# Two-layer decoder trunk on one core: expert positions in another order, overflow branch behind slot group 9 instead of 13

## Chip, cores and metric

One core of a Trainium2 chip runs the whole program. The metric is the device time of one execution in microseconds (us); the median of the runs is quoted. TensorE is PE in the profile (its weight loads PEld), VectorE DVE, ScalarE ACT, GpSimd POOL; SP is SyncE, whose queue issues all weight transfers here.

## The reference, cut to what matters

A trunk of two layers works on x (256 tokens x 1024). Layer 0 mixes with dilated attention and gated spatial mixing, layer 1 with a convolution module and stick-breaking attention; behind each mixer stands the same mixture of experts, and this is the part that the change touches:

```python
g_prob = softmax(x @ w_group + b_group)            # 4 groups, the best one is taken
e_val, e_idx = top_k(e_logits_of_that_group, 2)    # 2 of its 4 experts
gates = one_hot(group * 4 + e_idx) * (g_w * softmax(e_val))
for e in range(16):
    hid = silu(xt @ w_gate[e]) * (xt @ w_up[e])    # 1024 -> 512
    y = y + gates[:, e:e+1] * (hid @ w_down[e])    # 512 -> 1024
```

256 tokens with two experts each make 512 (token, expert) pairs for 16 experts. All is float32: the three matrices of one expert are 6 MB, those of both layers 192 MB.

## The kernel before

**Positions and slot groups.** The kernel sorts the experts of a layer by how many tokens chose them. Positions 0 and 1 are always experts 0 and 1 (`FIXED`), positions 2 to 15 the others, most chosen first. Each position has a fixed capacity of slots (`CAP`: 96 for positions 0 to 3, 64 for 4 to 7, 32 for 8 to 15; 896 in all). `_tasks()` goes through the positions and cuts their slots into slot groups of 64 or 32, 20 of them, numbered 0 to 19, and every 128 slots make a pack (7 packs). A position of 96 has two slot groups (64 and 32, or 32 and 64), the others have one each.

**A slot group** `i` goes through these steps, and the main loop of `moe_layer` overlaps neighbours: `prepare` copies its tokens into a window (ACT); `first_half` and `second_half` multiply the window with the gate and up matrices, 512 rows of them each (PE, L132 with `win` or `hs`); `hidden` makes silu(gate)*up*weight (ACT L1338, DVE L1339); `turn` transposes it (PE L1345, ACT L1347); `project` multiplies with the down matrix (PE, L132 with `ht`) and splits the result into two parts (ACT L1475, DVE L1476). When a pack is full, `combine` adds it to the tokens with matmuls (`ptt`, `yp`). Step `i` of the loop issues on PE: first half of `i+1`, `combine` where a pack has just ended, `turn` of `i`, second half of `i+1`, `project` of `i`.

**The ring of weights.** All big matrices of the program come as pieces of 1 MB (128 x 2048 float32) in a fixed order, `order`: four gate and up pieces and two down pieces for each position, 96 per expert layer. `moe()` writes this order from `TASKS`. The pieces go into 15 buffers (`raw`), and a few more tiles that are idle in this stage serve as buffers once (`pump_extra`). A piece is issued on SP (L248) when a buffer is free; a buffer is free when PE has done its last work with the piece, so the pieces of a position of 96 stay until its second slot group. SP issues in program order. The pieces of positions 0 and 1 can come before the routing is known; those of position 2 and on wait until the routing has told which expert stands there (L245).

**The overflow branch.** If an expert has more tokens than its capacity, the excess must be worked on apart. `whatever_is_left` reads the number of such tokens into a register of each engine (L1399) and goes into a branch (L1400) if it is over zero; the branch (`further`) loads the weights of that expert again, into tiles of its own. Its place is behind `project` of slot group `LEFT`, 13. In the profiled execution no engine goes into it, but each engine jumps past its code. In step 13 alone, `next_window` (the window copy of `i+2`, and the placing of its pack) stands behind the branch; in other steps it stands ahead of `project`.

Of the kernel before, what the change touches and what calls it, by code (L numbers as in the profile page):

```python
# [10 lines left out]
F32 = mybir.dt.float32  # L11
F32R = mybir.dt.float32r
# [7 lines left out]
P = 128  # L20
D = 1024
KD = 8
S = 256
# [13 lines left out]

FIXED = 2
CAP = (96,) * 4 + (64,) * 4 + (32,) * 8
PLAN = [[(0, 5), (1, 0), (1, 1)], [], [(1, 2), (1, 3), (1, 4), (1, 5)], []]  # L40
OD_ORDER = (0, 1, 2, 3, "2", 4, 5, 6, 7, "3", "4", 8, 9, "5", 10, 11, 12, 13)
HK = 1
# [2 lines left out]
AGE = 3  # L45
ADA_PE = {(0, 1), (1, 3), (1, 4), (1, 5)}
EXTRA = ("f8", "m8")
LEFT = 13
WARM = (1, 8, 8, 2, 4, 4, 3)


# [12 lines left out]
def _tasks():  # L64

    out, at = [], 0
    for p, cap in enumerate(CAP):
        base = 0
        while base < cap:
            n = 64 if cap - base >= 64 and at % 64 == 0 else 32  # L70
            out.append(dict(p=p, base=base, n=n, pack=at // P, row=at % P, first=base == 0, last=base + n == cap))
            base += n
            at += n
    assert at % P == 0
    return out


TASKS = _tasks()
# [31 lines left out]
def trunk_kernel(ctx: ExitStack, tc: tile.TileContext, a, out, dbg=None):  # L110
    nc = tc.nc
    V, A, G, T = nc.vector, nc.scalar, nc.gpsimd, nc.tensor
# [3 lines left out]
    sb = ctx.enter_context(tc.tile_pool(name="act", bufs=1))  # L116
# [5 lines left out]
    def bank(i):  # L122
        return pp.tile([P, 512], F32, name=f"b{i}", tag=f"b{i}")
# [327 lines left out]
    for i in range(4):  # L451
        b = bank(i)
# [820 lines left out]
    def place(rr, e, base, G):  # L1273

        pe = sb.tile([P, 2, P], BF, name="pe", tag="pt")
        for t in range(2):
            V.tensor_scalar(pe[:, t, :].rearrange("p (g w) -> p g w", g=G),
                            iota[:, 0:P // G].unsqueeze(1).to_broadcast([P, G, P // G]),
                            rr[:, t, e:e + 1], float(-base), op0=OP.subtract, op1=OP.is_equal)
        return pe  # L1280

    def moe_layer(l, then):
# [21 lines left out]
        with in_order():  # L1304
            g3, rr, hs, ofi, exi, pe = route(l, wa, cb, lg, th, tl, sm)

        def load_window(o, base, n):
            w = sb.tile([P, KD, n], F32, name="win", tag="sq", bufs=3)
            A.copy(w, hs[:, :, ds(o + base, n) if base else ds(o, n)])  # L1309
            return w  # L1310

        def slots(e, base, pe):
            b = bankbf(7)
            g = b[:, 512:518].bitcast(F32)
            for t in range(2):
                mm(g, pe[:, t, :], g3[:, t, e, :], start=(t == 0), stop=(t == 1))
            for t in range(2):
                T.transpose(b[:, t * P:(t + 1) * P], pe[:, t, :], identb)
            gs = sb.tile([P, 1], F32, name="gs", tag="gs1")
            V.tensor_reduce(gs, g, AX.X, OP.add)  # L1320
            ptt = sb.tile([P, S], F32R, name="ptt", tag="rs")
            A.copy(ptt, b[:, 0:S])
            return ptt, gs


        def gate_up(w, wts, b, G, halves=(0, 1)):
            n, r = DE // G, P // G
            for h in [x for f in halves for x in (2 * f, 2 * f + 1)]:
                i, src = h % 2, k3(wts[h], 4)
                for kk in range(4):  # L1330
                    for g in range(G):
                        mm(b[g * r:(g + 1) * r, i * n:(i + 1) * n], w[:, h // 2 * 4 + kk, :],
                           src[:, kk, g * n:(g + 1) * n], start=(h + kk == 0), stop=(h + kk == 6))

        def hidden(b, gs, G, tag="hid"):
            n = DE // G
            hid = sb.tile([P, n], F32, name="hid", tag=tag)
            A.activation(hid, b[:, 0:n], AF.Silu)  # L1338
            V.scalar_tensor_tensor(hid, hid, gs, b[:, n:2 * n], op0=OP.mult, op1=OP.mult)  # L1339
            return hid  # L1340

        def turn(hid, b, G, tag="ht"):
            n, m = DE // G, DE // G // P
            for c in range(m):
                T.transpose(b[:, c * P:(c + 1) * P], hid[:, c * P:(c + 1) * P], ident)  # L1345
            ht = sb.tile([P, m, G, P // G], F32, name="ht", tag=tag)
            A.copy(ht.rearrange("p c g s -> p (c g s)"), b[:, 0:n])  # L1347
            return ht

        def down(ht, wts, G):  # L1350
            n, r, m, q = D // G, P // G, DE // G // P, KD // G
            y = bank(6)
            for j in range(4):
                src = k3(wts[j // 2], 2)[:, j % 2, :].rearrange("p (n k) -> p n k", k=KD)
                for g in range(G):
                    mm(y[g * r:(g + 1) * r, 0:n], ht[:, j % m, j // m, :], src[:, :, q * g:q * (g + 1)],
                       start=(j == 0), stop=(j == 3))
            return y
# [5 lines left out]
        def further(p, base, bk):  # L1364

            def load(name, tag, cut):
                r = sb.tile([P, 2048], F32, name="raw", tag=tag)
                e = p if p < FIXED else nc.sync.value_load(exi[0:1, p:p + 1], min_val=0, max_val=NE - 1)
                nc.sync.dma_start(k3(r, 4 if name != "moe_w_down" else 2), cut(a[name][l, e]))
                return r  # L1370

            tags = ("f8", "m8", "m8b", "r8")
            wts = []
            for h in range(2):
                for name in ("moe_w_gate", "moe_w_up"):
                    wts.append(load(name, tags[len(wts)],
                                    lambda w: w.rearrange("(p k) n -> p k n", k=KD)[:, 4 * h:4 * h + 4, :]))
            b = bank(bk)
            pt, gs = slots(p, base, place(rr, p, base, 2))
            o = nc.scalar.value_load(ofi[0:1, 16 + p:17 + p], min_val=0, max_val=2 * S - base)  # L1380
            gate_up(load_window(o, base, 64), wts, b, 2)
            ht = turn(hidden(b, gs, 2, "m8b"), b, 2, "r8")
            wts = [load("moe_w_down", tags[h], lambda w: w.rearrange("(j p) n -> p j n", p=P)[:, 2 * h:2 * h + 2, :])
                   for h in range(2)]
            y = down(ht, wts, 2)
            for n in range(2):
                yx = sb.tile([P, 512], F32R, name="yx", tag="sq", bufs=3)
                A.copy(yx, y)
                if n:
                    V.tensor_sub(yx, y, yh.bitcast(F32))  # L1390
                yh = yx
                for kk in range(4):
                    for g in range(2):
                        k, rows = 4 * g + kk, slice(64 * g, 64 * g + 64)
                        mm(acc[k // 2][:, (k % 2) * S:(k % 2 + 1) * S],
                           yx.rearrange("p (n k) -> p k n", k=4)[rows, kk, :], pt[rows, :])
# [10 lines left out]
        start, banks, wins, gates, packs, hid, gu, dw_ = {}, {}, {}, {}, {0: pe}, {}, {}, {}  # L1407
        n = len(TASKS)

        def prepare(i):  # L1410
            t = TASKS[i]
            if t["p"] == 0:
                wins[i] = hs[:, :, t["base"]:t["base"] + t["n"]]
                return
            if t["first"]:
                start[t["p"]] = nc.scalar.value_load(ofi[0:1, 16 + t["p"]:17 + t["p"]], min_val=0, max_val=2 * S)
            wins[i] = load_window(start[t["p"]], t["base"], t["n"])
# [77 lines left out]
        for i, t in enumerate(TASKS):  # L1495
            if i + 1 < n:
                first_half(i + 1)
            if i and TASKS[i - 1]["pack"] < t["pack"]:
                combine(t["pack"] - 1)
            ht = turn(hid.pop(i), banks.pop(i), P // t["n"])  # L1500
            if i + 1 < n:
                gate_of(i + 1)
                second_half(i + 1)
            def next_window():
                if i + 2 < n:
                    prepare(i + 2)
                    j = TASKS[i + 2]["pack"]
                    if j > TASKS[i + 1]["pack"]:
                        packs.pop(j - 2, None)
                        packs[j] = place_pack(rr, j)  # L1510
                        return j

            if i != LEFT:
                j = next_window()
            project(i, ht)
            if i == LEFT:

                whatever_is_left(4 + i % 2)
                j = next_window()
            if j:  # L1520
                ptts[j] = turned_pack(j)
            if st["fin"]:
                ada_flush(7, -1)
# [14 lines left out]
    h = rms(drain_ada)  # L1538
# [81 lines left out]
```

## Time and profile before

| what | value |
|---|---|
| median of 3 runs | 855.37 us (850.36, 855.37, 857.51) |
| the profiled execution's own time | 853.71 us |
| its span, first to last instruction | 851.9 us (1.8 us lie around it) |
| PE busy | 710.1 us, 83% |
| DVE, ACT busy | 375.1 us (44%), 236.2 us (28%) |
| bytes moved by DMA | 288.11 MB, mean 338 GB/s |
| mean granted TensorE clock | 0.908 of 2.4 GHz |

Busy times of different engines overlap and don't add up to the span. The clock is granted at one of two levels, 1.2 or 2.4 GHz; a figure between is the mean of a stretch. The program runs in this order: layer 0 mixer to about 184 us, its experts to about 429 us, layer 1 mixer and routing to about 592 us, its experts to about 831 us, final norm and output.

### The profile page before, as it was taken

To read this page: it belongs to the slowest core of one execution; us is meant where nothing else is said; L and a number is where in the kernel's file an instruction comes from. 1 tells how busy PE (TensorE), PEld (TensorE's weight loads), DVE (VectorE), ACT (ScalarE), POOL (GpSimd) and SP (SyncE) were. 2 spreads that over 40 slices of the span, in tenths; PEclk is the share of its full clock that TensorE was granted. 3 is DMA by queue.
4 is the path that set the end of the run, shared out by engine and by line. 5 is a ranking of instruction groups with operands and counts; after the bars stand their busy time and mean duration, and the time that the engine had idled before them with its cause. 6 is when DMAs were issued, how large, how long until landed. Compare 5 with 4: busy or idle time off the path is not lost. (4 is left out here: it accounts for less than half of the span.)

```text
span 851.9 us, 18148 instructions
## 1 busy us (share of the span) xinstructions
PE 710.1 (83%) x7597; PEld 486.8 (57%) x7597; DVE 375.1 (44%) x852; ACT 236.2 (28%) x532; POOL 13.2 (2%) x33
## 2 busy tenths in 40 slices
PE   3699899889999997566638999997999999836666
PEld 2366369856665555443328887884666556524333
DVE  2435788883222122111157999997322212202113
ACT  3111241032232122211145336463222312111113
POOL 0000020000000000000000000000000000000000
PEclk9799999989999998775678999999999999976757
DMA  8999999949789999989999995501997699999981
GB/s 312 351 314 400 400 409 415 414 167 386 281 310 346 421 413 418 411 354 418 402 398 351 375 416 211 198 1 57 421 407 269 231 421 414 416 409 363 418 359 50
DMA packets 70027, 288.11 MB, mean 338 GB/s; under 512 B 8909, under 2 KB 11273, under 8 KB 53544
## 3 DMA queue, kind: packets, MB, share of 16 engines
q1 hardware_dynamic: 69928, 286.77, 85.6%
q8 instruction: 64, 1.05, 0.5%
q14 instruction: 35, 0.29, 0.1%
HBM read 285.69 MB, written 1.06 MB: 337 GB/s over the span
## 5 line engine op out<-in xcount | busy, mean ns | idle before, releaser
L132 PE MATMUL b<-raw,win 128*32 128x128 f32 (+1 forms) x3712 | 206.9, 323 | 36.2 <-ACT win L1309 19.1
L132 PEld LDWEIGHTS b<-raw,win 128*32 128x32 f32 (+1 forms) x3712 | 147.0, 126 | 88.7 <-ACT win L1309 20.5
L132 PE MATMUL b<-raw,ht 128*32 128x256 f32 (+1 forms) x1024 | 122.2, 505 | 28.8 <-DMA raw<-in_moe_w_down_dram 21.7
L1476 DVE TENSOR_TENSOR yp<-b,yp 32x256 fp32r<-32x256 f32 (+1 forms) x128 | 62.4, 488 | 166.9 <-ACT yp L1475 166.8
L1475 ACT CAST yp<-b 32x256 fp32r<-32x256 f32 (+1 forms) x128 | 53.5, 418 | 160.5 <-PE b L132 120.2
L132 PEld LDWEIGHTS b<-raw,ht 128*32 128x32 f32 (+1 forms) x1024 | 43.2, 128 | 87.6 <-issue 47.0
L310 DVE SCALAR_TENSOR_TENSOR raw<-raw,csil 128x1024 f32<-128x1024 f32 x56 | 74.6, 1332 | 4.2 <-DMA raw<-in_w_ada_dram 3.2
L1339 DVE SCALAR_TENSOR_TENSOR hid<-hid,gs,b 128x128 f32<-128x128 f32 (+1 forms) x40 | 16.0, 401 | 112.0 <-ACT hid L1338 111.9
L132 PE MATMUL b<-hh,whf 128*128 128x256 f32 x160 | 40.8, 294 | 13.2 <-ACT whf L601 13.1
L887 DVE SCALAR_TENSOR_TENSOR ac<-hqk,dw,ac 128x256 f32<-128x256 f32 x120 | 50.4, 476 | 0.2
L132 PE MATMUL b<-h,raw 128*128 128x256 f32 x192 | 44.9, 393 | 5.5 <-ACT h L574 2.9
L132 PEld LDWEIGHTS b<-h,raw 128*128 128x128 f32 x192 | 37.2, 197 | 13.3 <-ACT h L574 3.8
L1338 ACT ACTIVATE hid<-b 128x128 f32<-128x128 f32 (+1 forms) x40 | 12.8, 321 | 104.8 <-PE b L132 104.8
L132 PE MATMUL b<-mx,raw 128*128 128x256 f32 x160 | 40.8, 410 | 0.0
L132 PEld LDWEIGHTS b<-mx,raw 128*128 128x128 f32 x160 | 38.8, 335 | 1.5 <-issue 1.2
L132 PEld LDWEIGHTS b<-hh,whf 128*128 128x128 f32 x160 | 28.9, 194 | 17.5 <-ACT whf L601 15.2
L132 PE MATMUL b<-ptt,yp 128*128 128x256 f32 x224 | 34.3, 306 | 3.3 <-ACT yp L1475 3.1
L132 PE MATMUL b<-hl,whf 128*128 128x256 f32 x128 | 36.6, 286 | 0.0
L1437 DVE TENSOR_REDUCE gs<-b 128x1 f32<-128x3 f32 x40 | 6.4, 161 | 67.8 <-PE b L132 67.5
L132 PEld LDWEIGHTS b<-ptt,yp 128*128 128x128 f32 x224 | 30.2, 204 | 9.5 <-ACT yp L1475 6.0
L1347 ACT COPY ht<-b 128x128 f32<-128x128 f32 (+1 forms) x40 | 12.3, 309 | 77.3 <-PE b L1345 77.2
L132 PE MATMUL b<-raw,h 128*128 128x512 f32 x64 | 30.9, 631 | 0.0
(285 smaller groups left out, 821.4 us busy)
## 6 DMA issues: line engine op xcount, KB each, us to landing
raw<-in_moe_w_gate_dram SPq DMA_DIRECT2D x64, 1024.0 KB, 10.6
raw<-in_moe_w_up_dram SPq DMA_DIRECT2D x64, 1024.0 KB, 11.6
raw<-in_moe_w_down_dram SPq DMA_DIRECT2D x64, 1024.0 KB, 16.8
raw<-in_w_ada_dram SPq DMA_DIRECT2D x48, 1024.0 KB, 14.2
raw<-in_ev_w_in_dram SPq DMA_DIRECT2D x10, 1024.0 KB, 13.5
raw<-in_od_w_in_dram SPq DMA_DIRECT2D x10, 1024.0 KB, 8.3
raw<-in_ev_w_out_dram SPq DMA_DIRECT2D x4, 1024.0 KB, 16.0
raw<-in_od_w_out_dram SPq DMA_DIRECT2D x4, 1024.0 KB, 11.3
```

Source lines behind the costliest of these rows:

```text
L132: T.matmul(o, l, r, start=start, stop=stop, skip_group_check=True)
L310: ins = V.scalar_tensor_tensor(acc, src, csil[:, k:k + 1], acc, op0=OP.mult, op1=OP.add)
L887: V.scalar_tensor_tensor(ac[:, m, :], src, dw[:, m, j:j + 1], ac[:, m, :], op0=OP.mult, op1=OP.add)
L1338: A.activation(hid, b[:, 0:n], AF.Silu)
L1339: V.scalar_tensor_tensor(hid, hid, gs, b[:, n:2 * n], op0=OP.mult, op1=OP.mult)
L1347: A.copy(ht.rearrange("p c g s -> p (c g s)"), b[:, 0:n])
L1437: V.tensor_reduce(gates[i], g, AX.X, OP.add)
L1475: A.copy(yh[o[0], o[1], :], src)
L1476: V.tensor_sub(yl[o[0], o[1], :], src, yh[o[0], o[1], :].bitcast(F32))
```

## The change

`SEQ` gives the order in which the positions are worked on; `_tasks()` follows it, and with it the order of the pieces, the packs and the slot groups. There are 20 slot groups and 7 packs as before, of the same sizes. The new list of slot groups is, by position and size: 0 (64, 32), 1 (32, 64), 8 (32), 9 (32), 2 (64, 32), 10 (32), 3 (64, 32), 11, 12, 13 (32 each), 4, 5, 6, 7 (64 each), 14, 15 (32 each). `place_pack` writes a pack with one DVE instruction when all its positions are whole, equal and consecutive; that held for four packs before and holds for one in the new order, so the 7 packs take 19 such instructions per layer instead of 12.

The branch goes from behind slot group 13 to behind slot group 9, which is the first of position 3. `next_window` is gone: window copy and placing of a pack stand ahead of `project` in every step. Inside the branch the tiles are arranged anew, so that none of them is one of the windows' tiles.

```diff
--- before.py
+++ after.py
@@ -37,6 +37,8 @@
 
 FIXED = 2
 CAP = (96,) * 4 + (64,) * 4 + (32,) * 8
+
+SEQ = (0, 1, 8, 9, 2, 10, 3, 11, 12, 13, 4, 5, 6, 7, 14, 15)
 PLAN = [[(0, 5), (1, 0), (1, 1)], [], [(1, 2), (1, 3), (1, 4), (1, 5)], []]
 OD_ORDER = (0, 1, 2, 3, "2", 4, 5, 6, 7, "3", "4", 8, 9, "5", 10, 11, 12, 13)
 HK = 1
@@ -45,7 +47,7 @@
 AGE = 3
 ADA_PE = {(0, 1), (1, 3), (1, 4), (1, 5)}
 EXTRA = ("f8", "m8")
-LEFT = 13
+LEFT = 9
 WARM = (1, 8, 8, 2, 4, 4, 3)
 
 
@@ -64,7 +66,8 @@
 def _tasks():
 
     out, at = [], 0
-    for p, cap in enumerate(CAP):
+    for p in SEQ:
+        cap = CAP[p]
         base = 0
         while base < cap:
             n = 64 if cap - base >= 64 and at % 64 == 0 else 32
@@ -1304,8 +1307,8 @@
         with in_order():
             g3, rr, hs, ofi, exi, pe = route(l, wa, cb, lg, th, tl, sm)
 
-        def load_window(o, base, n):
-            w = sb.tile([P, KD, n], F32, name="win", tag="sq", bufs=3)
+        def load_window(o, base, n, tag=None):
+            w = sb.tile([P, KD, n], F32, name="win", tag=tag or "sq", bufs=1 if tag else 3)
             A.copy(w, hs[:, :, ds(o + base, n) if base else ds(o, n)])
             return w
 
@@ -1369,26 +1372,27 @@
                 nc.sync.dma_start(k3(r, 4 if name != "moe_w_down" else 2), cut(a[name][l, e]))
                 return r
 
-            tags = ("f8", "m8", "m8b", "r8")
+            tags = ("f8", "m8", "f8", "m8")
             wts = []
             for h in range(2):
                 for name in ("moe_w_gate", "moe_w_up"):
                     wts.append(load(name, tags[len(wts)],
                                     lambda w: w.rearrange("(p k) n -> p k n", k=KD)[:, 4 * h:4 * h + 4, :]))
-            b = bank(bk)
-            pt, gs = slots(p, base, place(rr, p, base, 2))
-            o = nc.scalar.value_load(ofi[0:1, 16 + p:17 + p], min_val=0, max_val=2 * S - base)
-            gate_up(load_window(o, base, 64), wts, b, 2)
-            ht = turn(hidden(b, gs, 2, "m8b"), b, 2, "r8")
+                if h == 0:
+                    b = bank(bk)
+                    pt, gs = slots(p, base, place(rr, p, base, 2))
+                    o = nc.scalar.value_load(ofi[0:1, 16 + p:17 + p], min_val=0, max_val=2 * S - base)
+                    w = load_window(o, base, 64, "m8b")
+                gate_up(w, wts, b, 2, (h,))
+            ht = turn(hidden(b, gs, 2, "r8"), b, 2, "m8b")
             wts = [load("moe_w_down", tags[h], lambda w: w.rearrange("(j p) n -> p j n", p=P)[:, 2 * h:2 * h + 2, :])
                    for h in range(2)]
             y = down(ht, wts, 2)
+            y2 = sb.tile([P, 2, 512], F32R, name="y2", tag="r8")
+            A.copy(y2[:, 0, :], y)
+            V.tensor_sub(y2[:, 1, :], y, y2[:, 0, :].bitcast(F32))
             for n in range(2):
-                yx = sb.tile([P, 512], F32R, name="yx", tag="sq", bufs=3)
-                A.copy(yx, y)
-                if n:
-                    V.tensor_sub(yx, y, yh.bitcast(F32))
-                yh = yx
+                yx = y2[:, n, :]
                 for kk in range(4):
                     for g in range(2):
                         k, rows = 4 * g + kk, slice(64 * g, 64 * g + 64)
@@ -1501,22 +1505,17 @@
             if i + 1 < n:
                 gate_of(i + 1)
                 second_half(i + 1)
-            def next_window():
-                if i + 2 < n:
-                    prepare(i + 2)
+            j = 0
+            if i + 2 < n:
+                prepare(i + 2)
+                if TASKS[i + 2]["pack"] > TASKS[i + 1]["pack"]:
                     j = TASKS[i + 2]["pack"]
-                    if j > TASKS[i + 1]["pack"]:
-                        packs.pop(j - 2, None)
-                        packs[j] = place_pack(rr, j)
-                        return j
-
-            if i != LEFT:
-                j = next_window()
+                    packs.pop(j - 2, None)
+                    packs[j] = place_pack(rr, j)
             project(i, ht)
             if i == LEFT:
 
                 whatever_is_left(4 + i % 2)
-                j = next_window()
             if j:
                 ptts[j] = turned_pack(j)
             if st["fin"]:
```

## Rows read from the trace of the kernel before

**Rows 1.** The page: the span.
```profile
span 851.9 us, 18148 instructions
```

**Rows 2.** Windows: stretch, length; busy PE, PEld, DVE, ACT, POOL; PEclk, DMA, GB/s.
```profile
219.00:288.00 69.00, 69.00 (x811) 41.61 (x809) 14.59 (x35) 16.68 (x42) 0.00 (x0) 1.00 0.86 330
...
362.00:385.00 23.00, 14.45 (x238) 9.17 (x241) 2.55 (x7) 2.57 (x8) 0.20 (x1) 0.75 0.91 360
...
448.00:592.00 144.00, 135.37 (x1029) 111.46 (x1029) 129.74 (x300) 71.30 (x135) 1.02 (x2) 0.99 0.59 228
...
631.00:682.00 51.00, 51.00 (x664) 31.37 (x664) 11.98 (x29) 13.95 (x35) 0.00 (x0) 1.00 0.74 279
682.00:744.00 62.00, 59.30 (x792) 36.64 (x788) 12.85 (x28) 12.70 (x31) 0.00 (x0) 1.00 1.02 416
...
765.00:795.00 30.00, 17.54 (x356) 12.85 (x355) 5.78 (x18) 4.30 (x13) 0.00 (x0) 0.75 0.95 380
795.00:828.00 33.00, 21.29 (x343) 12.19 (x339) 5.63 (x15) 5.36 (x17) 0.00 (x0) 0.66 1.01 409
```

**Rows 3.** Waits of SP in 631 to 682 us: total, times, longest.
```profile
SPq L248 <- PE b L132: 40.5, 11, 16.8
```

**Rows 4.** SP's timeline in layer 1: start, duration, issue of a piece.
```profile
631.17 0.33 SPq L248 DMA_DIRECT2D raw<-in_moe_w_up_dram  x1
644.44 0.33 SPq L248 DMA_DIRECT2D raw<-in_moe_w_gate_dram  x1
...
650.57 0.35 SPq L248 DMA_DIRECT2D raw<-in_moe_w_up_dram  x1
667.97 0.33 SPq L248 DMA_DIRECT2D raw<-in_moe_w_gate_dram  x1
```

**Rows 5.** ACT's timeline, layer 1: silu of slot groups 3, 4, 5, 9, 10, 11, 13, 14, 19.
```profile
631.17 0.38 ACT L1338 ACTIVATE hid<-b 128x256 f32<-128x256 f32 x1 [3.41 <-PE b L132]
...
642.73 0.39 ACT L1338 ACTIVATE hid<-b 128x256 f32<-128x256 f32 x1 [3.25 <-PE b L132]
...
650.58 0.28 ACT L1338 ACTIVATE hid<-b 128x128 f32<-128x128 f32 x1 [1.53 <-PE b L132]
...
692.40 0.39 ACT L1338 ACTIVATE hid<-b 128x256 f32<-128x256 f32 x1 [3.25 <-PE b L132]
...
703.69 0.38 ACT L1338 ACTIVATE hid<-b 128x256 f32<-128x256 f32 x1 [3.25 <-PE b L132]
...
716.55 0.39 ACT L1338 ACTIVATE hid<-b 128x256 f32<-128x256 f32 x1 [3.25 <-PE b L132]
...
733.98 0.28 ACT L1338 ACTIVATE hid<-b 128x128 f32<-128x128 f32 x1 [1.64 <-PE b L132]
...
740.41 0.28 ACT L1338 ACTIVATE hid<-b 128x128 f32<-128x128 f32 x1 [1.40 <-PE b L132]
...
819.50 0.28 ACT L1338 ACTIVATE hid<-b 128x128 f32<-128x128 f32 x1 [3.51 <-PE b L132]
```

**Rows 6.** Line L1400 in 740 to 790 us: ns min/median/max, first and last start.
```profile
L1400 SPq EVENT_SEMAPHORE  x7: 17/17/17, 766.3 to 780.9; - x7
L1400 PEldq COMPARE_BRANCH  x2: 81/3437/6793, 745.0 to 745.8; - x2
```

**Rows 7.** Timelines of SP and PE around the branch in layer 1.
```profile
784.36 1.03 SPq L248 DMA_DIRECT2D raw<-in_moe_w_down_dram  x2
...
755.41 2.78 PE L132 MATMUL b<-raw,win 128*32 128x128 f32 x45 [9.96 <-ACT win L1309]
```

**Rows 8.** PE's timeline in layer 0: half a slot group of 32 at either clock.
```profile
347.99 3.64 PE L132 MATMUL b<-raw,win 128*32 128x128 f32 x64 [9.13 <-ACT win L1309]
...
356.48 1.96 PE L132 MATMUL b<-raw,win 128*32 128x128 f32 x64
```

**Rows 9.** Timeline, 408 to 462 us: first issues and first use of layer 1's mixer weights.
```profile
403.96 16.41 SPq L248 DMA_DIRECT2D raw<-in_od_w_in_dram  x4
...
447.96 2.17 ACT L601 CAST whf<-raw 128x512 fp32r<-128x512 f32 x4
```

## Prediction

> **What bounds the kernel now.** I read the windows first, for the weight transfers and PE side by side, then SP's waits and its timeline, then the spacing of the slot groups on ACT, then the branch. A layer's experts need 96 pieces of 1.049 MB. Where nothing holds the transfers they run at 416 GB/s (682 to 744 [rows 2]), so a piece takes 1.049 MB / 416 GB/s = 2.52 us and a position (six pieces) 15.1 us, whatever its capacity.
>
> PE's price of a position depends on its capacity. The silu marks the end of a slot group's second half, so its spacing is PE's time per slot group [rows 5]: 740.41 - 733.98 = 6.4 us for a 32, 703.69 - 692.40 = 11.3 us for a 64, and 650.58 - 631.17 = 19.4 us for a position of 96 (two slot groups). A `combine` adds 12.9 - 11.3 = 1.6 us (716.55 - 703.69 against the spacing before it). So a 96 costs PE 4.3 us more than its transfer, a 64 costs 3.8 us less, a 32 costs 8.7 us less. All four 96s stand at the front. There the ring of buffers fills and SP waits for PE to empty one: of the 51 us from 631 to 682, SP waits 40.5 us for PE's matmuls [rows 3], and the issues stop from 631.17 to 644.44 and, after eight pieces (644.44 to 650.57), until 667.97 [rows 4]. PE is busy all the time, transfers run at 279 GB/s [rows 2]. Behind the 96s it turns round: transfers are full, PE waits for pieces, and the transfers set the end. So transfer time lost at the front is never made good. At 416 GB/s the loss is 51 x (1 - 279/416) = 16.8 us in layer 1, and 69 x (1 - 330/416) = 14.3 us in the same stretch of layer 0 (219 to 288) [rows 2]: 31.1 us together.
>
> **The change part by part.** *The order.* Number of pieces, slot groups, their sizes and PE's work stay. Slot groups 0 to 3 (positions 0, 1) are the same, so everything up to 631.17, the silu of slot group 3, should stand where it is. Then come positions 8 and 9, two 32s, instead of position 2. I follow the buffers in layer 1. Silu of slot group 4: 6.4 + 1.6 (a `combine` falls here) = 8.0 us later, 639; of slot group 5, a 32 that follows a projection of 64, 650.58 - 642.73 = 7.9 us [rows 5], 647. A piece of gate and up is free with its half of the matmuls, a piece of down with the projection behind. So by 649 free: four of position 8, two (down) of position 1, four of position 9, two of position 8: 12 pieces, the first about 636. Position 9's down and position 2's gate and up make 18 by about 665. Before, only eight were freed by then, and the next at 667.97 [rows 4]. The pieces issued up to 631.17 keep the queue busy to about 641 (four of 2.52 us from there), 12 more to 671, 18 to 686: the queue never runs dry. Afterwards position 2 and 10 take PE 19.4 + 6.4 = 25.8 us for 12 pieces that need 30.2 us, so do 3 and 11, and 12 and 13 are 32s: PE gains on the transfers all the time. I take off 31.1 us, and give back 1 us for a short hole that may be left about 640 in both layers: -30 us. The bounds of this term: all of it gone, and with it the holes at the branch (5.7 us, below), -37; or half of it left, -16.
>
> *Does PE become the bound?* From 631.2 PE has, in the new order, eight 32s (51 us), two 96s (39), four 64s (45), six `combine`s (9) and the branch (7): 151 us, so the last silu could stand at 783. The transfers allow it 16 to 17 us ahead of the 819.50 of before [rows 5], at about 803. The slack is 20 us; the end stays with the transfers, and the tail behind the last piece has the same two positions, 14 and 15, in it as before.
>
> *The branch* is moved past four slot groups. PE pays 6.8 us for its second compare-and-branch [rows 6] and stood 9.96 us in all, because the window copy came behind ACT's branch [rows 7]; with the window ahead of it I take 7. What is queued behind is slot group 11 and the buffers it frees; by then some six pieces (15 us) are queued or in flight, more than 7, so this hides. If that cover were gone it would cost 7 us a layer. On SP the branch waits from 766.3 until 780.9 for transfers in flight [rows 6], and SP issues again at 784.36 [rows 7], 3.4 us later. The transfers fall to 380 GB/s in 765 to 795 and 360 in 362 to 385 [rows 2]: a hole of 30 x (1 - 380/416) = 2.6 us and 23 x (1 - 360/416) = 3.1 us. All pieces behind are queued behind that wait. No row shows the branch where fewer transfers are in flight: at best the hole vanishes (-2.6 us a layer), at worst SP stands 3.4 us with nothing in flight and then the first piece takes its own 2.52 us: 6 us, 3.4 more than now. I take no difference, as the nearest rows, on both sides of the change, have a filled queue.
>
> *The rest.* `place_pack` has seven DVE instructions more per layer, DVE is busy 12 of 51 us there [rows 2], and PE needs the pack a slot group later: nothing. Without that cover, 7 x 0.41 us (11.98 us for 29 instructions) = 2.9 us a layer. The new tiles in the branch are not run.
>
> *Does layer 0's gain last?* Layer 1's mixer is bound by PE (135 of 144 us busy, transfers at 228 GB/s [rows 2]). Its first weights are issued from 403.96 on and first used at 447.96 [rows 9], so both its transfers and its start move ahead together with the end of layer 0's experts. I count it in full.
>
> Sum: 853.7 - 30 = 824 us for an execution like the profiled one (span 851.9 [rows 1], so about 822); the median shown is 1.7 us higher, within the spread of its own three runs. I predict 824.
>
> **The rivals.** (1) *The clock falls behind the 64s.* Positions 4 to 7 now stand where PE waits for pieces. In those stretches the granted clock averages 0.75 and 0.66, in the full ones 1.00 [rows 2], and at the lower level, 1.2 GHz, half a slot group of 32 took 3.64 instead of 1.96 us [rows 8], 1.86 times as much. At 1.86 a 64 costs 21.0 us and a 32 11.9: four 64s and the last two 32s lose 39 + 11 = 50 us, the last silu comes at 833 instead of 819.50, and the kernel takes 853.7 + 2 x 13.5 = 881 us. It turns slower from 20 + 17 = 37 us lost per layer, that is about three quarters of this stretch at the lower level. For it: such means were measured there. Against it: they were measured with PE busy 18 of 30 and 21 of 33 us; 64s ask for 11.3 of 15.1 us at the full clock, all of it at the lower one, and stretches with 59.3 of 62 us busy or more had 1.00 [rows 2]. The Trainium skill ("TensorE: Matmul & The Clock Gate", section "HAM oscillation — how this bites in real kernels") speaks for this rival: it says that PE whose bursts alternate with long waits for DMA is throttled again and again and starts each burst at the low clock. By that rule alone the 881 would stand; the trace agrees with it for 32s and has no 64 in such a stretch.
>
> (2) *The branch costs in its new place.* If the queue is short at that time, PE's 7 us and SP's hole add up to 7 us a layer, so half the gain: 853.7 - 16 = 838. For it: it comes where PE has just left the front. Against it: the count of 18 pieces by 665.
>
> (3) *The gain stays in one layer,* because the mixer between absorbs it: 853.7 - 16 = 838. Against it: the order of events above.
>
> (4) *The change does not do what it says:* the transfers lose the same time elsewhere, because the ring refills with later pieces while something else on PE (evacuation at the pack ends, say) holds the buffers: 853 to 856. Against it: rows 3 put the waits on matmuls.
>
> **How the numbers follow.** The forecast gets 0.72, rival 1 0.08, rival 2 0.10, rival 3 0.04, rival 4 0.06. The forecast's own range is 817 to 831 (-37, to -30 with 3.4 us a layer given back at the branch). Rivals 1 and 4 are left out (0.14); with rivals 2 and 3 in, and 2 us at either end because single runs differ by that much and more, the range that should hold 8 in 10 is 815 to 840. A change under 1% (8.5 us) is about what a measurement of this kernel can't tell from none. Faster by over 1% are the forecast, rivals 2 and 3: 0.86; the same, rival 4: 0.06; slower, rival 1: 0.08.
>
> **What would show it.** The forecast is right if the stretch that follows slot group 3 runs at 405 GB/s or more in both layers, SP's waits for matmuls there shrink to a few us, PE first waits for pieces only from position 4 or 5 on, and routing of layer 1 comes some 14 us earlier. Rival 1 shows as a clock near 0.5 in positions 4 to 7 with PE full and SP waiting for it again. Rival 2 shows as a dip of the transfers right at the branch. The step that I trust least is the count of freed buffers about 640: if slot groups 4 and 5 come later than 649, holes remain.

## The result and the profile after

The changed kernel took 824.05 us (median of 4 runs, 823.33 to 827.35), the kernel before 852.96 in the runs beside it: ratio 0.9663, 95% interval 0.9607 to 0.9719. The profiled execution has a span of 821.9 us, 30.0 less than [rows 1]. So the forecast of 824 holds, and the 30 us can be followed by stage.

The windows of the changed kernel (columns as in [rows 2]) in the order of time, layer 0 first; the stretches 219 to 274 and 617 to 668 answer to 219 to 288 and 631 to 682 of before:

```profile
219.00:274.00 55.00, 54.75 (x915) 35.79 (x913) 13.93 (x40) 15.03 (x41) 0.00 (x0) 1.00 1.02 415
274.00:312.00 38.00, 30.23 (x621) 21.86 (x618) 8.35 (x21) 9.38 (x26) 0.00 (x0) 0.91 0.94 374
...
617.00:668.00 51.00, 50.77 (x882) 33.67 (x876) 13.75 (x38) 14.71 (x40) 0.00 (x0) 1.00 1.02 409
668.00:692.00 24.00, 15.35 (x250) 10.19 (x247) 4.93 (x13) 4.24 (x11) 0.00 (x0) 0.85 1.01 410
692.00:712.00 20.00, 19.18 (x427) 14.73 (x430) 4.89 (x14) 5.66 (x16) 0.00 (x0) 0.84 0.87 348
712.00:730.00 18.00, 18.00 (x221) 10.71 (x215) 4.98 (x15) 5.61 (x15) 0.00 (x0) 1.00 1.02 415
730.00:751.00 21.00, 19.45 (x142) 10.25 (x140) 2.58 (x6) 3.59 (x9) 0.00 (x0) 1.00 1.02 416
751.00:781.00 30.00, 22.47 (x256) 11.98 (x253) 3.82 (x8) 3.88 (x9) 0.00 (x0) 1.00 1.02 416
```

Behind slot group 3 the transfers are full: 415 GB/s for 330 and 409 for 279 [rows 2]. PE is as busy there as before (54.75 of 55 and 50.77 of 51 us). What is left is one dip per layer, at the branch (374 and 348).

SP's timeline shows that the long stops of [rows 4], 13.3 and 17.4 us, are gone: the longest left is 8.8 us, from 635.06 to 643.85 (start, duration, issue; first the first piece behind the routing, then pieces that follow slot group 3):

```profile
577.59 0.35 SPq L251 DMA_DIRECT2D raw<-in_moe_w_gate_dram  x1
...
619.82 0.35 SPq L251 DMA_DIRECT2D raw<-in_moe_w_gate_dram  x1
...
635.06 0.33 SPq L251 DMA_DIRECT2D raw<-in_moe_w_up_dram  x1
643.85 3.24 SPq L251 DMA_DIRECT2D raw<-in_moe_w_down_dram  x4
650.52 0.35 SPq L251 DMA_DIRECT2D raw<-in_moe_w_gate_dram  x1
```

ACT's silus of slot groups 3, 4, 5 and 19 of layer 1 answer to [rows 5]:

```profile
616.96 0.38 ACT L1341 ACTIVATE hid<-b 128x256 f32<-128x256 f32 x1 [3.41 <-PE b L135]
625.58 0.28 ACT L1341 ACTIVATE hid<-b 128x128 f32<-128x128 f32 x1 [1.53 <-PE b L135]
633.23 0.28 ACT L1341 ACTIVATE hid<-b 128x128 f32<-128x128 f32 x1 [1.69 <-PE b L135]
...
789.53 0.28 ACT L1341 ACTIVATE hid<-b 128x128 f32<-128x128 f32 x1 [3.82 <-PE b L135]
```

In the kernel before, the first piece of position 2 in layer 1, which marks the end of the routing, went out here (SP's timeline):

```profile
591.85 0.36 SPq L248 DMA_DIRECT2D raw<-in_moe_w_gate_dram  x1
```

So layer 1's routing ends 591.85 - 577.59 = 14.3 us earlier, which is layer 0's part. From there to the last silu the kernel before took 819.50 - 591.85 = 227.7 us [rows 5], the changed one 789.53 - 577.59 = 211.9, which is 15.7 us less. Together this is the 30.0 us of the span.

### The profile page after: what moved, and what is told of

Its sections match the earlier page's. It is cut to its first block, busy times and chain, and to the rows that moved or that the text cites. A ratio compares the mean times of both kernels' runs of the same rounds, so it can differ in the third digit from the quotient of the medians.

```text
span 821.9 us, 18157 instructions
## 1 busy us (share of the span) xinstructions
PE 703.7 (86%) x7597; PEld 485.0 (59%) x7597; DVE 375.6 (46%) x866; ACT 236.1 (29%) x532; POOL 13.2 (2%) x33
## 5 line engine op out<-in xcount | busy, mean ns | idle before, releaser
L135 PE MATMUL b<-raw,win 128*32 128x128 f32 (+1 forms) x3712 | 200.3, 310 | 35.5 <-issue 17.9
L135 PEld LDWEIGHTS b<-raw,win 128*32 128x32 f32 (+1 forms) x3712 | 142.4, 121 | 85.5 <-issue 27.3
L135 PE MATMUL b<-raw,ht 128*32 128x256 f32 (+1 forms) x1024 | 116.8, 475 | 19.3 <-DMA raw<-in_moe_w_down_dram 13.2
L135 PE MATMUL b<-ptt,yp 128*128 128x256 f32 x224 | 36.4, 306 | 3.9 <-ACT yp L1479 2.9
L1350 ACT COPY ht<-b 128x128 f32<-128x128 f32 (+1 forms) x40 | 12.3, 308 | 86.6 <-PE b L1348 86.5
## 6 DMA issues: line engine op xcount, KB each, us to landing
raw<-in_w_ada_dram SPq DMA_DIRECT2D x48, 1024.0 KB, 14.3
```

The lines of the kernel that those rows point to most:

```text
L135: T.matmul(o, l, r, start=start, stop=stop, skip_group_check=True)
```

## The experiments

All of them start from the changed kernel, and each ratio is to the kernel before, in runs on the same chip.

**The order alone.**

```diff
-LEFT = 9
+LEFT = 13
```

> The new order with the branch back behind slot group 13. Theory (the ring, held by PE in the front, starved the transfers; the order alone cures it): 821 to 827 us, the stretch behind slot group 3 as full as in the changed kernel, a branch hole of 2 to 4 us a layer at the new-old place. Rival (the place of the branch brought the gain): 840 us or more.

826.49 us, ratio 0.964 (0.9585 to 0.9696), which can't be told from the changed kernel. The hole of the transfers at the branch, now behind slot group 13, is there as expected: 352 GB/s in 345 to 365 and 357 in 742 to 764, which is 3.1 us a layer. Its window behind slot group 3 of layer 1:

```profile
620.00:671.00 51.00, 50.77 (x882) 33.78 (x882) 13.75 (x38) 14.75 (x40) 0.00 (x0) 1.00 1.01 409
```

**The branch alone.**

```diff
-SEQ = (0, 1, 8, 9, 2, 10, 3, 11, 12, 13, 4, 5, 6, 7, 14, 15)
+SEQ = tuple(range(16))
```

> The old order with the branch behind slot group 9 and everything else as changed. Theory: 849 to 856 us, no better than before, with 279 GB/s again in the stretch behind slot group 3 of layer 1. Rival (the place of the branch): 822 to 835 us.

859.73 us, ratio 1.0044 (1.0012 to 1.0076): above the band that was expected, no gain, rather a touch of loss. The same window:

```profile
635.50:686.50 51.00, 51.00 (x662) 31.37 (x662) 11.97 (x29) 14.06 (x35) 0.00 (x0) 1.00 0.74 278
```

With these two the gain is the order's, and the branch's place brings none of it.

**No branch.** The call of `whatever_is_left` is taken out.

```diff
-            if i == LEFT:
-                whatever_is_left(4 + i % 2)
```

> The changed kernel without the overflow branch (tokens over a position's capacity would be left out; there are none here). Theory (the holes of 3.8 and 3.3 us at the branch lie on the path, PE's 6 us do not): 815 to 819 us, transfers at 415 GB/s through slot group 9. Rival (the queued pieces hide the branch): 822 to 826 us.

824.92 us, ratio 0.9611 (0.9538 to 0.9685): the median misses the band, and the interval holds both the theory's number and no change. The trace tells more than the time. The stretches that had 374 and 348 GB/s:

```profile
274.00:312.00 38.00, 35.49 (x755) 25.38 (x751) 9.29 (x24) 10.78 (x30) 0.00 (x0) 1.00 1.02 416
...
692.00:712.00 20.00, 18.69 (x370) 13.61 (x364) 6.04 (x19) 6.02 (x17) 0.00 (x0) 1.00 1.01 413
```

So the dip belongs to the branch, and it is worth 38 x (1 - 374/416) = 3.8 us in layer 0 and 20 x (1 - 348/416) = 3.3 us in layer 1. From the first to the last silu of a layer, this kernel takes 195.5 us (203.15 to 398.61) and 191.8 us (598.81 to 790.56), the changed one 197.1 (200.85 to 397.93) and 194.9 (594.64 to 789.53): 4.8 us less in the two. In the profiled executions it lost 2.3 us ahead of the first silu and 3.5 us between the layers, in stages that the edit doesn't touch, and that is as large as the effect. The price of the branch on the whole time stays open between nothing and some 5 us.

**Small positions first.**

```diff
+SEQ = (0, 1, 8, 9, 10, 11, 12, 13, 14, 15, 4, 5, 6, 7, 2, 3)
```

> The changed kernel with positions 0, 1, 8 to 15, 4 to 7, 2, 3: all small ones first, the two 96s last. Theory (transfers must be fed, and PE must not be left with work behind the last piece): transfers are full from slot group 3 on and the last piece lands at about the same time as in the changed kernel, but PE ends some 11 us a layer later, 838 to 850 us. Rival (any order that breaks up the run of 96s is worth the same): 822 to 828 us.

843.61 us, ratio 0.9841 (0.9788 to 0.9893). The transfers are full behind slot group 3, and stop early at the end, while PE goes on (windows):

```profile
629.00:717.00 88.00, 63.91 (x1375) 46.86 (x1375) 19.13 (x54) 19.46 (x56) 0.00 (x0) 0.86 1.02 414
...
790.00:845.00 55.00, 43.14 (x532) 24.91 (x528) 14.77 (x32) 15.67 (x34) 0.00 (x0) 0.89 0.41 165
```

In the first stretch PE was busy for 63.91 of 88 us; it waited 7.8 us for pieces, and 10.7 us are its two stops at the branch (6.77 and 3.89), which falls into this stretch here. The 96s then keep it full from 790 to 800 and 806 to 812, and when the last pieces land, most of the last 96 is still to do: the last silu comes 225.3 us behind the end of the routing (590.16 to 815.47), for 211.9 in the changed kernel. So no run of 96s at the front is not enough: large ones at the end give the time back as PE's work.

**The price of a 96 cut, order old (layer 1).** `left_only`, and in layer 1 the 32-slot group of each 96 leaves out 11 of 16 gate and up steps and 2 of 4 down steps.

```diff
-                for kk in range(4):
+                for kk in ((0, 3) if cut and h == 3 else (0,) if cut else range(4)):
...
-            for j in range(4):
+            for j in ((0, 3) if cut else range(4)):
```

with `cut = l and t["n"] < 64 < CAP[p]` at the three calls in the main loop.

> The old order (branch behind slot group 9, as in left_only), but in layer 1 alone the 32-slot group of each position of 96 does only 5 of its 16 gate and up steps and 2 of its 4 down steps (its output is not the reference's). PE's price of a 96 falls by about 3.7 us, from 19.4 to 15.7, near the 15.1 us of its pieces; the order of the pieces stays. Theory (PE's time in the 96s holds the buffers): the stretch behind slot group 3 of layer 1 gains, some 12 to 15 us of layer 1 vanish: 840 to 848 us, and layer 0 keeps its hole. Rival (the gain comes from the order of the pieces itself, not from PE's time): 853 us or more.

848.0 us, ratio 0.9938 (0.9899 to 0.9977), at the upper end of the band. The order of the pieces is the old one, and yet the stretch behind slot group 3 goes from 278 to 355 GB/s, because PE empties buffers sooner:

```profile
630.50:681.50 51.00, 49.10 (x483) 28.40 (x478) 13.35 (x31) 15.12 (x37) 0.00 (x0) 1.00 0.92 355
```

That is 51 x (355 - 278)/416 = 9.4 us of transfers; against `left_only`, which ran on another chip, the ratio to the kernel before fell by 0.0106, 9 us. The theory asked for 12 to 15, and the hole didn't close: it is the right mechanism, and the price of a 96 fell less than planned, to 16.2 and 17.8 us (silus at 630.47, 646.70 and 664.48), which is still above 15.1 and leaves part of the hole.

**The same cut, order new.**

> The changed kernel with the same work left out in layer 1. Theory: the transfers set the end already, so only 3 to 6 us at the start of layer 1's experts are left to gain: 817 to 822 us, while old_cut gains 12 to 15. Rival (PE is the bound in the new order): 810 us or less.

823.2 us, ratio 0.9622 (0.9581 to 0.9663), by the ratios 3.5 us below the changed kernel, with intervals that overlap. The stretch was full already and stays so:

```profile
618.50:669.50 51.00, 49.54 (x812) 31.86 (x810) 14.24 (x39) 15.75 (x43) 0.00 (x0) 1.00 1.02 413
```

Less work for PE is worth 9 us in the old order, and in the new one 3.5 us that are not clear of the noise. The traces say the same of the way from the end of the routing to the last silu: 219.2 us (595.84 to 815.05) for 230.8 (595.52 to 826.27) in the old order, 210.6 (582.85 to 793.48) for 211.9 in the new one. So PE is not the bound in the new order, and PE's time in the 96s was what held the old one.

**32s last.** Positions 4 to 7 ahead of 12 and 13.

```diff
+SEQ = (0, 1, 8, 9, 2, 10, 3, 11, 4, 5, 6, 7, 12, 13, 14, 15)
```

> The changed kernel with positions 4 to 7 ahead of 12 and 13 (order 0, 1, 8, 9, 2, 10, 3, 11, 4, 5, 6, 7, 12 to 15). Theory (behind position 11 the transfers are full whatever comes): 821 to 828 us, the last piece of each layer lands when it did; the granted clock of the last 70 us of a layer's experts falls from 0.9 to about 0.75, since 32s leave PE waiting, without harm. Rival (64s near the end keep the clock up and that is part of the gain): 831 us or more.

826.07 us, ratio 0.9669 (0.9626 to 0.9713). Layer 1's 751 to 781, with 32s now, had a clock of 0.85 for the 1.00 of the changed kernel, at nearly the same busy time, and full transfers in both:

```profile
751.00:781.00 30.00, 21.65 (x370) 13.55 (x366) 4.39 (x11) 3.94 (x11) 0.00 (x0) 0.85 1.02 415
```

Over 730 to 800 the clock was 0.87 against 0.91, a smaller fall than the 0.75 that was expected. Between these two orders of what stands behind position 11 no difference shows, and none from the clock there.

**One small position between.**

```diff
+SEQ = (0, 1, 8, 2, 3, 9, 10, 11, 12, 13, 4, 5, 6, 7, 14, 15)
```

> The changed kernel with one 32 instead of two between positions 1 and 2, and none between 2 and 3 (order 0, 1, 8, 2, 3, 9 to 13, 4 to 7, 14, 15). Theory, by the count of freed buffers: with positions 2 and 3 in a row the transfers run dry once, for some 14 us in each layer: 845 to 853 us. Rival (any small position in between is worth its share): 834 to 840 us.

844.64 us, ratio 0.9898 (0.9863 to 0.9934), 0.4 us below the theory's band and well away from the rival's. SP issues as in [rows 4] again, with one long stop, and the window is in between (SP's timeline, then the window):

```profile
647.92 0.33 SPq L251 DMA_DIRECT2D raw<-in_moe_w_up_dram  x1
666.87 2.10 SPq L251 DMA_DIRECT2D raw<-in_moe_w_down_dram  x2
```

```profile
627.00:678.00 51.00, 50.88 (x797) 32.23 (x797) 12.89 (x35) 13.85 (x37) 0.00 (x0) 1.00 0.78 316
```

51 x (1 - 316/416) = 12.3 us are lost, for some 14 expected and 16.8 in the old order: one small position brought back about a quarter. So what counts is how long PE is behind the transfers in a row, not whether the order is mixed at all.

## Why the prediction was right, step by step

**The order, -31.1 + 1 us.** Measured by the same windows: 14.3 us of layer 0's hole are gone (415 GB/s), and 51 x (409 - 279)/416 = 15.9 us of layer 1's. Size and mechanism hold; `seq_only` and `left_only` put it on the order, `old_cut`, `new_cut` and `one_small` on PE's time in the 96s.

**The count of freed buffers was wrong.** The silus of slot groups 4 and 5 came 8.6 and 16.3 us behind that of slot group 3, for 8.0 and 15.9 predicted. But by then the prediction had 12 pieces issued (649 in its clock, 18 us behind silu 3); the trace has eight up to 635.06, 18.1 us behind, and the next four at 643.85. The ring was not what the prediction took it for: four of the tiles that serve as buffers are lent once (`r8`, `m8b`, `f8`, `m8`), by the code they hold pieces of positions 8 and 9 in the new order, and when those are done nothing is issued into them. 12 less four are the eight. That these four are the missing ones is read from the code and the count; it wasn't tried apart. The conclusion stood on a thinner margin than was claimed. Four pieces in flight (the prediction's figure) and eight more are 12 x 2.52 = 30 us behind 616.96, which is 647, and the next issue came at 643.85: about 3 us to spare, where the prediction had over 20. The transfers in 40 slices of 617 to 668 us show how near it was:

```profile
GB/s 414 414 411 414 405 405 431 430 418 411 418 418 424 411 418 418 418 418 424 424 424 363 273 402 373 382 363 392 395 411 450 437 424 392 411 443 411 424 411 424
```

The 273 stands at 645 to 646. This small dip is 51 x (1 - 409/416) = 0.9 us, the hole of 1 us that the prediction gave back: its size came right by luck, since the reason wasn't in the count.

**A sign that failed.** SP's waits for matmuls were to shrink to a few us in this stretch. They did not (SP's waits in 617 to 668: total, times, longest):

```profile
SPq L251 <- PE b L135: 29.5, 16, 8.2
```

That is 29.5 us for 40.5 [rows 3], and yet the transfers were full. So the total of the waits does not tell whether the transfers starve. The longest wait fits better: 8.2 us here for 16.8 before, which what was queued and in flight could cover.

**PE as the bound.** The slack holds: apart from the branch PE first waits for a piece at 735.5, for position 6, where the prediction said from position 4 or 5 on, and `new_cut` gains little. The last silu came 789.53 - 616.96 = 172.6 us behind that of slot group 3, for 172 that the transfers and 152 that PE alone would have allowed by the prediction.

**The branch.** "No difference" was nearly right: 3.8 and 3.3 us of holes for 3.1 and 2.6, 1.4 us more in all, inside the bounds that were given. The cover held as well: while PE stood, the transfers went on at 410 GB/s (668 to 692), so the queue hid PE's stop. Its size was right in layer 0 (6.87 us for the 7 taken), but in layer 1 PE stood twice (PE's timeline; the 42 matmuls between are the first part of a half slot group):

```profile
687.26 2.74 PE L135 MATMUL b<-raw,win 128*32 128x128 f32 x42 [6.53 <-issue]
692.69 1.50 PE L135 MATMUL b<-raw,win 128*32 128x128 f32 x22 [2.70 <-issue]
```

That is 9.2 us, nearly as much as before (9.96 [rows 7]), though the window stood ready. The term that was mis-sized is SP's (the semaphores at the branch, then SP's next issue):

```profile
L1404 SPq EVENT_SEMAPHORE  x7: 17/17/17, 678.3 to 688.9; - x7
...
694.05 1.15 SPq L251 DMA_DIRECT2D raw<-in_moe_w_down_dram  x2
```

SP waited for its transfers until 688.9 and issued again 5.1 us later, where the prediction had 3.4 from the kernel before; in layer 0 it was 298.0 to 302.50, 4.5 us, for 4.0 before. It hardly waited for PE in this time (0.2 us in layer 1, none in layer 0), so PE's stop did not make the hole. The pieces that were left in flight ran out instead: 115 GB/s in 692 to 694, 37 in 694 to 696, 406 in the 2 us behind. No run took the branch from one engine alone.

**Layer 0's gain lasts:** 14.3 us at the end of layer 1's routing. Rival 3 is out.

**Rival 1, the clock.** It did not come: positions 4 to 7 run at 1.00, with PE 22.47 of 30 us busy where it waits most (751 to 781, positions 7 and 14). `thirtytwos_last` has the lower clock in that stretch with the smaller slot groups. The Trainium skill ("TensorE: Matmul & The Clock Gate", section "HAM oscillation — how this bites in real kernels") has PE throttled again and again where long waits for DMA stand between its bursts. That this did not bite agrees with the waits being short here: the longest in 751 to 781 was 1.6 us. But the longest was 1.6 us also in 795 to 822 of the kernel before, with 32s, and there the clock was 0.69; so the length of the waits alone does not tell the two apart, and why the 64s keep the clock stays open. No run put 64s into much longer waits.

**Rival 2** is seen as a dip at the branch, at 3.3 to 3.8 us a layer, most of which the kernel before paid as well, and not at the 7 us more that the rival asked for. **Rival 4** falls with the result: outside the dips the transfers run at 409 GB/s or more in the windows shown, so the time was not lost elsewhere.

## What to carry to other kernels

Where weights stream through a ring of buffers and the work on a piece varies, compare for each item the time that the computing engine holds its pieces with the time that they take to load. The order should never leave the engine behind the transfers by more than the ring holds, and never leave it with the large items behind the last load; one small item between large ones may be too little. Behind the critical stretch, swapping small and middle items made no difference here. When buffers are counted, tiles that are lent only once are not part of the ring.

## What was not expected of the hardware

Jumping past the branch's code cost PE 6.87 us in layer 0 and 6.53 us in layer 1 of the changed kernel, with nothing to wait for in the profile. In layer 1 PE ran 42 matmuls and stood again for 2.70 us; the granted clock averaged 0.84 in 692 to 712, where 617 to 668 and 712 to 730 had 1.00. `thirtytwos_last` and `one_small` have such a second stop in layer 1 too (2.70 and 2.66 us). But `no_branch` has stops of 2.14 and 1.19 us without a visible cause as well (before 301.46 and 697.67), so it isn't shown that the second stop is the branch's. SP needed 4.5 and 5.1 us from its last semaphore to its next issue. Without the branch the stops of over 6 us and the dips of the transfers were not there, and the clock was 1.00 in 692 to 712.
